# The end of a decoder layer on one Trainium2 core: the first half of the output written during the last product's steps, and the last three steps ordered by blocks of tokens

## The chip, the cores and the metric

The kernel runs on one core of a Trainium2 chip. The metric is the device time of one execution in microseconds; before the change the median of three runs is 2199.48 us (2195.65 to 2199.91). The profile comes from a further execution.

## The reference

One decoder layer over 512 tokens of width 2048 in float32: two groups of attention heads with a residual, then a SwiGLU feed-forward block with a residual. Only its last two lines matter here:

```
h = rmsnorm(x, g_pre_ffn[l]) * (1.0 + sc_f) + sh_f
f = (jax.nn.silu(h @ w_gate[l]) * (h @ w_up[l])) @ w_down[l]
x = x + gt_f * rmsnorm(f, g_post_ffn[l])
```

So the last product, by `w_down` (5632 x 2048), is followed by a mean of squares over all 2048 columns of a token, by a gain for each column, and by the residual. No element of a token's output can be written before all its columns are there.

## The kernel before

**Precision.** Every float32 operand of a product is split in two: `hi`, a rounded copy (ScalarE, line 1704), and `lo`, what is left (VectorE, line 1713). A product is three matmuls: activations hi by weights hi, hi by lo, lo by hi (lines 282 to 284). The matmul by `hi` of a step can therefore start before its `lo` is there, the next one can't.

**Steps.** All the work after the first stage is a list of steps, each with one 128x1024 tile of weights (512 KB). In step `i` the program issues on each engine, in this order: what was hung on the step's start, the step's first half of matmuls, `do_hi(i + 2)` on ScalarE, the second half of matmuls, what was hung on `post_ev`, `do_lo(i + 2)` on VectorE, then `post_end`, `d_sums` (sums of weight tiles on VectorE) and `d_load` (loads on SyncE's queue, line 1505 for activations, 1522 for weights). Each engine runs its own instructions strictly in that order. `w_hi` and `w_lo` have three buffers each, so `do_hi(i + 2)` waits until step `i - 1` has been read by TensorE.

**The last product.** Its 512 x 5632 by 5632 x 2048 is done by one level of a Strassen-like scheme with seven products instead of eight, for two halves `c` of the columns. Tokens are four blocks of 128: blocks 0 and 1 are the first token half, 2 and 3 the second. For each `c` the products come as `m1`, `P`, `R`, `Y2`, then `Q` and `m2` in turn, and at last `T`, eleven steps each. `dpos[c, name, j]` is the number of a step.  A step works on two blocks of tokens (`tb` 0 and 1) with 6 matmuls each, so it has 12 matmuls. With `N` the number of steps, the last eleven, `N-11` to `N-1`, are `T` of `c = 1`; step `N-12` is `m2, 10`. `T` adds only to the second token half of the second half of the columns (`q = 2`), so the first token half is complete after `m2`.

**Finishing.** `du` holds the product's rows in SBUF, one tile for each block of tokens. `d_copy` and `d_comb` (lines 1608, 1612) bring in PSUM's sums, `d_sq` (1625, ScalarE) squares with a sum over 512 columns, `rstd` (1152 to 1157; VectorE, then GpSimd) makes the factor of a token, `d_gain` (1630, VectorE) multiplies by the gains, and `d_out` (1654) does `du * rstd + x2` on VectorE and starts the write to DRAM (1655, mostly on SyncE's queue). `x2`, the residual, is read back from DRAM by `x2_load` (1659), into buffers `XTAGS` that hold weights until then.

**Order at the end.** The matmuls of the last `NLAST = 2` steps are kept back and ordered by blocks of tokens:

```
last = range(NSTEP - NLAST, NSTEP)
for tb in range(2):
    for q in range(2):
        d_out(tb, 1024 * q, 1024)
for tb in range(2):
    for i in last:
        steps[i]["mm"](*hl[i], tb)
    d_comb(1, 2, "R", OP.add, (tb,))
    ...
```

The four `d_out` of the first token half (128x1024 each) stand on VectorE behind the last `w_lo` and ahead of everything that the second half needs.

Of the kernel before, what the change touches and what calls it, by code (L numbers as in the profile page):

```python
# [34 lines left out]
def body(tc, t):  # L35
# [5 lines left out]
    with ctx:  # L41
# [272 lines left out]
        start_ev = defaultdict(list)  # L314
        pe_ev = defaultdict(list)
        mid_ev = defaultdict(list)
        post_ev = defaultdict(list)
# [341 lines left out]
        post_end = defaultdict(list)  # L659
# [288 lines left out]
        dseq, dpos = [], {}  # L948
# [31 lines left out]
        NSTEP = len(steps)  # L980
# [75 lines left out]
        for i in range(W0 + 60):  # L1056
# [24 lines left out]
            while ada_todo and i < W0 + 46 and i >= 1 and t_dve + 1.14 <= t_end + (M_ADA if i < W0 else M_ADAW) and \  # L1081
                    t_dma + 1.45 <= t_end + M_DMA and len(aux[i]) < NAUX:
                t_dma += 1.45
                n, ch, hf = ada_todo.pop(0)
# [42 lines left out]
        HF = {}  # L1127
# [21 lines left out]
        def rstd(ss, n):  # L1149

            if n > 1:
                dve.reduce_sum(ss[:, 5:6], ss[:, 0:n], axis=mybir.AxisListType.X)
                src = ss[:, 5:6]
            else:
                src = ss[:, 0:1]
            dve.tensor_scalar(ss[:, 6:7], src, 1.0 / D, EPS, op0=OP.mult, op1=OP.add)
            pool.tensor_tensor(ss[:, 7:8], ss[:, 6:7], mhalf[:, 0:1], op=OP.pow)
# [339 lines left out]
        def d_load(e):  # L1497
            while aloads and aloads[0][0] <= e:
                c, name, j = aloads[0][1:]
                p = apool.get()  # L1500
                assert p is not None, (e, aloads[0])
                aloads.pop(0)
                a_of[c, name, j] = p
                v = p[1].rearrange("p (h k t) -> p h k t", h=2, k=2)
                sync.dma_start(v, acts[ACOMBO[DP[name][0]], j])
                atile[c, name, j] = v.bitcast(R)
            while dloads and dloads[0][0] <= e:
                at, end, c, n, q, j = dloads[0]
                p = None
                if c == 1 and n == "C":  # L1510
                    p = rawp.get([u for u in ("raw", "R10", "R11", "P2", "P5", *STAGE_RAW) if u not in XTAGS])
                elif c == 1:
                    p = rawp.get(XTAGS)
                if p is None:
                    p = rawp.get()
                if p is None:
                    assert end > e, (e, dloads[0], len(apool.free))
                    break
                dloads.pop(0)
                draw_of[c, n, j] = p  # L1520
                draw[c, n, j] = p[1]
                sync.dma_start(p[1], adar[dots[j]] if n == "dot" else wds[c, q, j])
# [97 lines left out]
        def d_sq(c, q, tbs=(0, 1)):  # L1620
            if "t" not in sq:
                sq["t"] = U("R7", [128, 4, 512], name="sq")
            for tb in tbs:
                t_, cg = 2 * (q // 2) + tb, 2 * c + q % 2
                act.activation(sq["t"][:, tb, :], du(c, q, tb), AF.Square, accum_out=HF["dss", t_][:, cg:cg + 1])

        def d_gain(c, q, tbs=(0, 1)):
            for tb in tbs:
                u = du(c, q, tb)
                dve.tensor_tensor(u, u, GTG[1][:, 2 * c + q % 2, :], op=OP.mult)  # L1630

        for c in range(2):
            p = dpos
            post_ev[p[c, "m1", 10] + 1].append(lambda c=c: d_copy(c, 0, "m1"))
            post_ev[p[c, "P", 10] + 1].append(lambda c=c: d_copy(c, 3, "P"))
            post_ev[p[c, "Y2", 10] + 1].append(lambda c=c: d_c12(c))
            post_ev[p[c, "Y2", 10] + 2].append(lambda c=c: d_comb(c, 3, "R", OP.subtract))
            post_ev[p[c, "Q", 10] + 1].append(lambda c=c: (d_copy(c, 2, "m1"), d_comb(c, 1, "m1", OP.subtract)))
            post_ev[p[c, "m2", 10] + 1].append(lambda c=c: d_comb(c, 0, "m2", OP.add))
            post_ev[p[c, "m2", 10] + 2].append(lambda c=c: d_comb(c, 3, "m1", OP.subtract))  # L1640
            post_ev[p[c, "m2", 10] + 3].append(lambda c=c: (d_sq(c, 0), d_sq(c, 1)))
            post_ev[p[c, "m2", 10] + 4].append(lambda c=c: d_sq(c, 3))
            if c == 0:
                post_ev[p[c, "T", 10] + 1].append(lambda c=c: d_comb(c, 2, "R", OP.add))
                post_ev[p[c, "T", 10] + 2].append(lambda c=c: d_sq(c, 2))
# [1 line left out]
        for n, (c, q) in enumerate(((0, 0), (0, 1), (0, 2), (0, 3))):  # L1647
            post_end[gtf_end + 8 + 2 * n].append(lambda c=c, q=q: d_gain(c, q))
        for n, q in enumerate((0, 1, 3)):
            post_end[dpos[1, "m2", 10] + 5 + n].append(lambda q=q: d_gain(1, q))  # L1650

        def d_out(tb, c0, n):
            u = HF["du", tb].rearrange("p c n -> p (c n)")[:, c0:c0 + n]
# [3 lines left out]
        def x2_load(tb):  # L1657
            HF["x2", tb] = U(XTAGS[tb], [128, 2048], name=f"x2_{tb}")
            sync.dma_start(HF["x2", tb], x2d[tb])
        for tb in range(4):  # L1660
            start_ev[dpos[1, "T", 0] + 1 + tb].append(lambda tb=tb: x2_load(tb))
        for tb in range(2):
            post_end[NSTEP - 4].append(lambda tb=tb: rstd(HF["dss", tb], 4))


        LA = 2
# [100 lines left out]
            do_hi(i)  # L1767
            do_lo(i)

        NLAST = 2  # L1770
        for i in range(NSTEP):
            for f in start_ev[i]:
                f()
# [39 lines left out]
                d_more()  # L1813

        last = range(NSTEP - NLAST, NSTEP)
        for tb in range(2):
            for q in range(2):
                d_out(tb, 1024 * q, 1024)
        for tb in range(2):
            for i in last:  # L1820
                steps[i]["mm"](*hl[i], tb)
# [107 lines left out]
```

## Time and profile before

| | |
|---|---|
| median of 3 runs | 2199.48 us (2195.65 to 2199.91) |
| the profiled execution | 2196.76 us |
| its span, first to last instruction | 2195.0 us |
| TensorE busy (matmuls) | 2152.4 us, 98% |
| VectorE busy | 1668.9 us, 76% |
| ScalarE busy | 1058.3 us, 48% |
| GpSimd busy | 107.1 us, 5% |
| mean granted TensorE clock | 0.993 of full speed |

The span lies 1.76 us under the profiled execution's own time. Busy shares are means over the whole span; what holds the end is read from the last 45 us, step by step. A timeline row gives the start, the duration, engine, line, operation, what it writes and reads with the shape, the number of instructions merged in the row, and in brackets the idle time of the engine before it and who ended it. Rows of one engine overlap by some hundredths: the next VectorE instruction starts about 0.08 us before the row of the one ahead of it ends.

### The profile page before, as it was taken

Reading aid. Unit: us, or ns where it says so; the run is one execution under the profiler, and the core shown is the slowest. Engines: PE = TensorE matmul, PEld = TensorE weight load, DVE = VectorE, ACT = ScalarE, POOL = GpSimd, SP = SyncE. Lnnn points to the kernel's source line nnn. Section 1 sums busy time; section 2 is a strip of 40 time slices with the busy share of each in tenths; the row PEclk is TensorE's granted clock in tenths of the full one; section 3 lists DMA queues with packets and bytes.
Section 4 is the critical chain, followed back from the end, with each engine's and each line's share of the span. In section 5 each row is a group of like instructions: output and inputs, shape, how many; then the busy total and the mean of one; then the engine's idle time right before and its main releaser. Section 6 shows DMA issues by size and latency. Waiting matters only on the chain.

```text
span 2195.0 us, 26915 instructions
## 1 busy us (share of the span) xinstructions
PE 2152.4 (98%) x9748; PEld 1757.8 (80%) x9748; DVE 1668.9 (76%) x2333; ACT 1058.3 (48%) x1541; POOL 107.1 (5%) x116
## 2 busy tenths in 40 slices
PE   7999999999999999999999999999999999999997
PEld 6888777778888888777888888888888888888886
DVE  6987877776777676776777777776777788798888
ACT  5444344444435564644555554555555544444443
POOL 0000000001001000000001001000000000000000
PEclk8999999999999999999999999999999999999999
DMA  9797534545678877897778769778877889899996
GB/s 374 295 347 228 165 119 150 176 160 166 217 230 274 294 248 252 274 294 220 222 233 268 225 205 289 213 206 262 244 222 214 278 322 401 335 387 363 345 338 266
DMA packets 161028, 566.48 MB, mean 258 GB/s; under 512 B 17504, under 2 KB 17792, under 8 KB 154496
## 3 DMA queue, kind: packets, MB, share of 16 engines
q1 hardware_dynamic: 142608, 502.09, 63.8%
q0 software_dynamic: 11520, 41.95, 10.7%
q10 hardware_dynamic: 6768, 20.73, 3.1%
q8 instruction: 77, 1.26, 0.2%
q14 instruction: 55, 0.45, 0.1%
HBM read 501.77 MB, written 54.02 MB: 253 GB/s over the span
## 4 chain that ended last, share of the span: by engine, by line
PE 88%; DVE 5%; DMA 4%; ACT 1%; issue 1%; SPq 0%; POOL 0%; POOLq 0%; ACTq 0%; DVEq 0%
PE b L283 22%; PE b L282 22%; PE b L284 22%; PE b L277 6%; PE b L279 5%; PE b L278 5%; PE b L507 2%; DVE w_lo L1713 2%; DMA a<-acts 1%; PE b L545 1%; DMA raw<-in_wgu 1%; PE b L1276 1%; PE b L500 1%; PE b L529 1%; ACT w_hi L1704 1%
## 5 line engine op out<-in xcount | busy, mean ns | idle before, releaser
L1713 DVE TENSOR_TENSOR w_lo<-raw,w_hi 128x1024 fp32r<-128x1024 f32 x232 | 282.7, 1222 | 140.9 <-ACT w_hi L1704 140.7
L1704 ACT ACTIVATE w_hi<-raw 128x1024 fp32r<-128x1024 f32 x232 | 245.6, 1060 | 291.7 <-PE b L284 216.8
L282 PE MATMUL b<-w_hi,h 128*128 128x512 f32 x864 | 343.7, 398 | 2.3 <-ACT w_hi L1704 2.0
L283 PE MATMUL b<-w_lo,h 128*128 128x512 f32 x864 | 337.9, 391 | 4.1 <-DVE w_lo L1713 4.0
L284 PE MATMUL b<-w_hi,h 128*128 128x512 f32 x864 | 337.5, 391 | 0.0
L1713 DVE TENSOR_TENSOR w_lo<-w_raw,w_hi 128x1024 fp32r<-128x1024 f32 x176 | 214.2, 1221 | 61.3 <-ACT w_hi L1704 61.1
L1704 ACT ACTIVATE w_hi<-w_raw 128x1024 fp32r<-128x1024 f32 x176 | 185.2, 1055 | 142.7 <-PE b L284 58.3
L282 PE MATMUL b<-w_hi,e 128*128 128x512 f32 x640 | 249.9, 390 | 3.2 <-ACT w_hi L1704 3.2
L283 PE MATMUL b<-w_lo,e 128*128 128x512 f32 x640 | 250.1, 391 | 1.6 <-DVE w_lo L1713 1.6
L284 PE MATMUL b<-w_hi,e 128*128 128x512 f32 x640 | 249.7, 390 | 0.0
L283 PE MATMUL b<-w_lo,a 128*128 128x512 f32 x616 | 240.0, 390 | 1.1 <-DVE w_lo L1713 1.1
L282 PE MATMUL b<-w_hi,a 128*128 128x512 f32 x616 | 240.1, 390 | 1.0 <-DMA a<-acts 1.0
L284 PE MATMUL b<-w_hi,a 128*128 128x512 f32 x616 | 239.7, 389 | 0.0
L1704 ACT ACTIVATE w_hi<-w_lent 128x1024 fp32r<-128x1024 f32 x128 | 135.7, 1061 | 165.8 <-PE b L284 125.2
L1713 DVE TENSOR_TENSOR w_lo<-w_lent,w_hi 128x1024 fp32r<-128x1024 f32 x128 | 156.3, 1223 | 76.7 <-ACT w_hi L1704 76.7
L277 PE MATMUL b<-h,w_hi 128*128 128x512 f32 x512 | 213.3, 417 | 0.0
L278 PE MATMUL b<-h,w_hi 128*128 128x512 f32 x512 | 200.8, 392 | 2.5 <-DVE h L273 2.5
L279 PE MATMUL b<-h,w_lo 128*128 128x512 f32 x512 | 201.3, 393 | 0.0
L283 PEld LDWEIGHTS b<-w_lo,h 128*128 128x128 f32 x864 | 162.8, 188 | 39.8 <-DVE w_lo L1713 6.7
L282 PEld LDWEIGHTS b<-w_hi,h 128*128 128x128 f32 x864 | 162.6, 188 | 39.6 <-issue 3.7
L284 PEld LDWEIGHTS b<-w_hi,h 128*128 128x128 f32 x864 | 162.6, 188 | 34.2
L282 PEld LDWEIGHTS b<-w_hi,e 128*128 128x128 f32 x640 | 120.5, 188 | 28.5 <-ACT w_hi L1704 3.6
(348 smaller groups left out, 3448.1 us busy)
## 6 DMA issues: line engine op xcount, KB each, us to landing
a<-acts SPq DMA_DIRECT2D x154, 512.0 KB, 5.5
raw<-in_wgu SPq DMA_DIRECT2D x127, 512.0 KB, 6.6
w_raw<-in_win SPq DMA_DIRECT2D x107, 512.0 KB, 5.0
w_raw<-in_adar SPq DMA_DIRECT2D x96, 512.0 KB, 4.5
w_lent<-in_wgu SPq DMA_DIRECT2D x73, 512.0 KB, 6.2
w_raw<-in_wout SPq DMA_DIRECT2D x64, 512.0 KB, 4.8
raw<-in_wgu POOLq DMA_DIRECT2D x56, 512.0 KB, 7.0
raw<-in_wds SPq DMA_DIRECT2D x46, 512.0 KB, 6.2
```

The lines of the kernel that those rows point to most:

```text
L277: pe.matmul(ps, whi, ahi, start=start, stop=False, **kw)
L278: pe.matmul(ps, whi, alo, start=False, stop=False, **kw)
L279: pe.matmul(ps, wlo, ahi, start=False, stop=stop, **kw)
L282: pe.matmul(ps, ahi, whi, start=start, stop=False, **kw)
L283: pe.matmul(ps, ahi, wlo, start=False, stop=False, **kw)
L284: pe.matmul(ps, alo, whi, start=False, stop=stop, **kw)
L500: pe.matmul(sc[:, r], qk[:, i, qs], qk[:, i + 1, :N], start=True, stop=True)
L507: pe.matmul(sc[:, :N], qk[k, 2 * m, qs], qk[k, 2 * m + 1, :N], start=True, stop=True)
L529: pe.transpose(tr[:, j, :], misc["p"][:, n % 2, 128 * j:128 * j + 128], ident)
L545: pe.matmul(h["pv"][:, qb, :], d["pt"][:, o:o + 128], v[:, j, e], start=j == 0, stop=j == qb)
L1704: act.activation(hi, raw, AF.Copy)
L1713: dve.tensor_tensor(lo, raw, hi.bitcast(F), op=OP.subtract)
```

## The change

The diff does six things. `d_sq` of the product's first three quarters moves one step earlier, for both `c`. `d_gain(1, q)` moves two steps earlier, to steps `N-9`, `N-8`, `N-7`. `rstd` of blocks 0 and 1 moves from step `N-4` to `N-9`. The four `d_out` of the first token half leave the end and are hung on steps `N-7`, `N-6`, `N-5` and `N-4`, each behind that step's `do_lo`. The four loads of `x2` move from steps `N-10` to `N-7` to steps `N-22`, `N-20`, `N-18` and `N-16`; for that, late loads of weights take other buffers than `XTAGS`. Three steps instead of two are kept back and ordered by blocks of tokens.

```diff
-                elif c == 1:
+                elif c == 1 and n in ("B12", "B22"):
                     p = rawp.get(XTAGS)
+                elif at > dpos[1, "m2", 0] - 8:
+                    p = rawp.get([u for u in ("raw", "R10", "R11", "P2", "P5", *STAGE_RAW) if u not in XTAGS])
...
-            post_ev[p[c, "m2", 10] + 3].append(lambda c=c: (d_sq(c, 0), d_sq(c, 1)))
-            post_ev[p[c, "m2", 10] + 4].append(lambda c=c: d_sq(c, 3))
+            post_ev[p[c, "m2", 10] + 2].append(lambda c=c: (d_sq(c, 0), d_sq(c, 1)))
+            post_ev[p[c, "m2", 10] + 3].append(lambda c=c: d_sq(c, 3))
...
-            post_end[dpos[1, "m2", 10] + 5 + n].append(lambda q=q: d_gain(1, q))
+            post_end[dpos[1, "m2", 10] + 3 + n].append(lambda q=q: d_gain(1, q))
...
-            start_ev[dpos[1, "T", 0] + 1 + tb].append(lambda tb=tb: x2_load(tb))
+            start_ev[dpos[1, "m2", 5 + tb]].append(lambda tb=tb: x2_load(tb))
...
-            post_end[NSTEP - 4].append(lambda tb=tb: rstd(HF["dss", tb], 4))
+            post_end[dpos[1, "m2", 10] + 3].append(lambda tb=tb: rstd(HF["dss", tb], 4))
+            for q in range(2):
+                post_end[dpos[1, "m2", 10] + 5 + 2 * tb + q].append(lambda tb=tb, q=q: d_out(tb, 1024 * q, 1024))
...
-        NLAST = 2
+        NLAST = 3
...
-        for tb in range(2):
-            for q in range(2):
-                d_out(tb, 1024 * q, 1024)
```

The first place where instructions move is VectorE, up to the first `d_comb` of the end. `w_lo` is the splitting of a step's weights, `du_13991` and `du_13994` are blocks 0 and 1, `du_14070` and `du_14073` blocks 2 and 3, `gtg` the gains, `x_0` and `x_1` the residuals. Before, from the last but one `w_lo` on:

```order
L1713 TENSOR_TENSOR w_lo<-stage_7304,w_hi 128x1024
L1152 TENSOR_REDUCE dss<-dss 128x1
L1156 TENSOR_SCALAR dss<-dss 128x1
L1152 TENSOR_REDUCE dss<-dss 128x1
L1156 TENSOR_SCALAR dss<-dss 128x1
L1713 TENSOR_TENSOR w_lo<-w_lent,w_hi 128x1024
L1654 SCALAR_TENSOR_TENSOR du_13991<-du_13991,dss,x_0_16024 128x1024 x2
L1654 SCALAR_TENSOR_TENSOR du_13994<-du_13994,dss,x_1_16047 128x1024 x2
L1612 TENSOR_TENSOR du_14070<-du_14070,b_14806 128x512
```

And now, from the first output on:

```order
L1656 SCALAR_TENSOR_TENSOR du_13991<-du_13991,dss,x_0_15792 128x1024
L1717 TENSOR_TENSOR w_lo<-stageb,w_hi 128x1024
L1632 TENSOR_TENSOR du_14070<-du_14070,gtg_15898 128x512
L1632 TENSOR_TENSOR du_14073<-du_14073,gtg_15898 128x512
L1656 SCALAR_TENSOR_TENSOR du_13991<-du_13991,dss,x_0_15792 128x1024
L1717 TENSOR_TENSOR w_lo<-stage_6928,w_hi 128x1024
L1656 SCALAR_TENSOR_TENSOR du_13994<-du_13994,dss,x_1_15831 128x1024
L1717 TENSOR_TENSOR w_lo<-stage_7304,w_hi 128x1024
L1656 SCALAR_TENSOR_TENSOR du_13994<-du_13994,dss,x_1_15831 128x1024
L1717 TENSOR_TENSOR w_lo<-w_lent,w_hi 128x1024
L1614 TENSOR_TENSOR du_14070<-du_14070,b_14806 128x512
```

The four outputs, which stood behind the last `w_lo`, now stand one ahead of each of the last four (steps `N-4` to `N-1`), and two gains stand among them as before.

The second place is SyncE's queue at the end; `a` are activations, `x` the residual, `out` the output. Before:

```order
L1659 DMA x_3_16093<-x2d 128x2048
L1505 DMA a_13090<-acts 128x1024 x2
L1655 DMA out<-du_13991 128x1024 x2
L1655 DMA out<-du_13994 128x1024 x2
L1655 DMA out<-du_14070 128x512 x4
```

And now:

```order
L1661 DMA x_3_15917<-x2d 128x2048
L1505 DMA a_13091<-acts 128x1024
L1505 DMA a_13089<-acts 128x1024 x2
L1505 DMA a_13090<-acts 128x1024 x2
L1505 DMA a_13091<-acts 128x1024 x2
L1505 DMA a_13089<-acts 128x1024 x2
L1657 DMA out<-du_13991 128x1024
L1505 DMA a_13090<-acts 128x1024
L1657 DMA out<-du_13991 128x1024
L1505 DMA a_13090<-acts 128x1024
L1657 DMA out<-du_13994 128x1024 x2
```

The activations of steps `N-2` and `N-1` (`a_13090`, two halves of one buffer) now stand each behind a write of the output.

## Rows read from the trace of the kernel before

**Rows 1.** The page's head: the span, and each engine's busy time with its share and number of instructions.

```profile
span 2195.0 us, 26915 instructions
PE 2152.4 (98%) x9748; PEld 1757.8 (80%) x9748; DVE 1668.9 (76%) x2333; ACT 1058.3 (48%) x1541; POOL 107.1 (5%) x116
```

**Rows 2.** Busy time by windows of one step each (from one `w_hi` to the next; steps `N-10` and `N-9`, `N-6` to `N-3`, and the end): window and length, busy time of PE, PEld, DVE, ACT and POOL with their instructions, the granted clock, the share of the DMA engines, GB/s.

```profile
2153.61:2156.38 2.77, 2.77 (x13) 2.06 (x11) 2.77 (x4) 1.06 (x1) 0.00 (x0) 1.00 1.01 413
2156.38:2159.80 3.42, 3.05 (x14) 2.42 (x14) 3.42 (x6) 3.42 (x9) 0.00 (x0) 1.00 1.04 426
...
2165.16:2167.88 2.72, 2.72 (x13) 2.25 (x12) 2.66 (x4) 1.06 (x2) 0.00 (x0) 1.00 1.00 413
2167.88:2170.60 2.72, 2.72 (x13) 2.25 (x12) 2.72 (x5) 1.07 (x2) 0.00 (x0) 1.00 0.87 343
2170.60:2173.32 2.72, 2.72 (x13) 2.25 (x12) 2.72 (x5) 1.06 (x2) 0.00 (x0) 1.00 0.04 17
2173.32:2176.04 2.72, 2.72 (x13) 2.25 (x12) 2.11 (x7) 1.06 (x1) 1.08 (x2) 1.00 0.00 0
2176.04:2181.50 5.46, 5.40 (x24) 4.13 (x22) 4.98 (x5) 0.45 (x1) 0.00 (x0) 1.00 0.71 284
```

**Rows 3.** VectorE's timeline over the last 46 us.

```profile
2149.75 1.28 DVE L1612 TENSOR_TENSOR du<-du,b 128x512 f32<-128x512 f32 x2 [1.98 <-ACT du L1608]
...
2155.62 1.22 DVE L1713 TENSOR_TENSOR w_lo<-rawR,w_hi 128x1024 fp32r<-128x1024 f32 x1
...
2157.95 1.22 DVE L1713 TENSOR_TENSOR w_lo<-w_lent,w_hi 128x1024 fp32r<-128x1024 f32 x1
...
2160.29 1.23 DVE L1713 TENSOR_TENSOR w_lo<-stage,w_hi 128x1024 fp32r<-128x1024 f32 x1
...
2173.28 0.15 DVE L1152 TENSOR_REDUCE dss<-dss 128x1 f32<-128x4 f32 x1
...
2173.72 0.15 DVE L1156 TENSOR_SCALAR dss<-dss 128x1 f32<-128x1 f32 x1
2174.41 1.23 DVE L1713 TENSOR_TENSOR w_lo<-w_lent,w_hi 128x1024 fp32r<-128x1024 f32 x1 [0.54 <-ACT w_hi L1704]
2175.55 4.87 DVE L1654 SCALAR_TENSOR_TENSOR du<-du,dss,x 128x1024 f32<-128x1024 f32 x4
2180.34 0.68 DVE L1612 TENSOR_TENSOR du<-du,b 128x512 f32<-128x512 f32 x1
2185.85 0.68 DVE L1612 TENSOR_TENSOR du<-du,b 128x512 f32<-128x512 f32 x1
...
2188.71 2.74 DVE L1654 SCALAR_TENSOR_TENSOR du<-du,dss,x 128x512 f32<-128x512 f32 x4 [0.44 <-POOL dss L1157]
```

**Rows 4.** TensorE's timeline: the first matmul of step `N-9` and the next one, the first of step `N-3`, the first of the two steps kept back, the last of their first block of tokens, and the last of all.

```profile
2156.13 0.39 PE L282 MATMUL b<-w_hi,a 128*128 128x512 f32 x1
2156.89 0.50 PE L283 MATMUL b<-w_lo,a 128*128 128x512 f32 x1 [0.37 <-DVE w_lo L1713]
...
2173.12 0.39 PE L282 MATMUL b<-w_hi,a 128*128 128x512 f32 x1
...
2175.84 0.39 PE L282 MATMUL b<-w_hi,a 128*128 128x512 f32 x1
...
2178.33 0.39 PE L284 MATMUL b<-w_hi,a 128*128 128x512 f32 x1
...
2181.05 0.39 PE L284 MATMUL b<-w_hi,a 128*128 128x512 f32 x1
```

**Rows 5.** DMAs from issue to landing, shortest, median and longest: the activations over 2085 to 2196 us, the same over 2120 to 2150 us, and the writes of the output.

```profile
DMA to landing us min/median/max: 3.4/5.7/9.2
...
DMA to landing us min/median/max: 3.4/4.9/6.8
...
DMA to landing us min/median/max: 2.2/2.4/2.9
```

**Rows 6.** Busy time by windows, columns as in rows 2: the stretch of steps `N-23` to `N-17`, the one in which the residual is loaded before the change, and the one between the last load and the first write.

```profile
2118.10:2137.10 19.00, 19.00 (x86) 15.60 (x85) 15.10 (x19) 7.57 (x8) 0.00 (x0) 1.00 0.88 321
...
2151.00:2162.50 11.50, 11.13 (x50) 8.89 (x49) 11.50 (x15) 7.77 (x17) 0.00 (x0) 1.00 0.93 360
2170.60:2176.90 6.30, 6.30 (x29) 5.22 (x28) 5.69 (x11) 2.12 (x2) 1.08 (x2) 1.00 0.02 7
```

**Rows 7.** ScalarE's timeline where it writes the row of gains to DRAM and waits for it, and the `w_lo` behind that on VectorE.

```profile
2133.46 0.33 ACTq L1021 DMA_DIRECT2D rowd<-row  x1
...
2136.17 1.06 ACT L1704 ACTIVATE w_hi<-stage 128x1024 fp32r<-128x1024 f32 x1 [2.73 <-DMA rowd<-row]
...
2137.26 1.23 DVE L1713 TENSOR_TENSOR w_lo<-stage,w_hi 128x1024 fp32r<-128x1024 f32 x1 [2.11 <-ACT w_hi L1704]
```

**Rows 8.** TensorE's clock near the start: windows of 2 us (columns as in rows 2), the wait ahead of a transpose that falls among them, and two matmuls at the lower clock.

```profile
16.00:18.00 2.00, 0.00 (x0) 0.00 (x0) 1.27 (x7) 1.79 (x4) 0.55 (x1) 0.50 1.06 436
30.00:32.00 2.00, 0.73 (x6) 0.41 (x4) 2.00 (x4) 1.80 (x4) 0.00 (x0) 1.00 1.02 418
...
18.08 1.97 PE L207 MATMUL b<-cst,x_in 128*128 128x128 f32 x8 [4.10 <-DVE x_in L135]
...
25.23 0.63 PE L277 MATMUL b<-h,w_hi 128*128 128x512 f32 x1
25.65 0.63 PE L278 MATMUL b<-h,w_hi 128*128 128x512 f32 x1
```

## The prediction

> **What bounds the kernel now.** I read the page first: TensorE is busy for 2152.4 of 2195.0 us, VectorE for 76% [rows 1]. By that mean VectorE has room for anything. The change touches only the last 75 us, so next come windows of one step each: in steps N-10 and N-9 VectorE is busy for the whole window, and from N-6 to N-4 for 2.66 to 2.72 of 2.72 us [rows 2]. Here VectorE has no room. In the same rows TensorE loses time only in N-9 (3.05 busy of 3.42 us). Then VectorE's timeline [rows 3]: from 2149.75 on it waits for next to nothing (11.50 busy of 11.50 us up to 2162.5 [rows 6], 0.06 us free in N-6), then for 0.54 us on the last `w_hi`; the four outputs of the first token half follow (2175.55, 4.87 us in all), and at 2180.34 the first `d_comb` of the second half. TensorE ended that block's matmuls at 2178.33 + 0.39 = 2178.72 and all of them at 2181.44 [rows 4]. So the end is VectorE's: block 2 waits 1.6 us for it, block 3 4.4 us. From `d_comb` to `d_comb` is 5.51 us (2180.34 to 2185.85), the second chain ends at 2191.45, and the span 3.55 us later, with the last write and the closing. That the end hangs on VectorE is what invites the change. What the reader is to see is that the place to which the work goes is VectorE's as well.
>
> **The change, part by part.**
>
> *The outputs on VectorE.* Four of about 1.20 us each (2175.55 to 2180.34) leave the end and come ahead of the last four `w_lo`. The work between 2149.75 and the last `w_lo` is otherwise the same, only its order changes: two pairs of gains and the two `rstd` come earlier. Where VectorE has no idle time, order does not change when a list of work is done. I follow the new order with the row's own pitches: `w_lo` 1.14 (2174.41 to 2175.55), a pair of `du` operations 1.20 (2155.62 to 2157.95 holds one and a `w_lo`), two `rstd` 0.6 (2173.28 to 2173.87). Up to `w_lo` of N-7 at 2160.29 nothing changes. Then gains 2161.43, `rstd` 2162.63, `w_lo` N-6 2163.25, four gains, `w_lo` N-5 2166.8, gains, output, `w_lo` N-4 2170.3, gains, output, `w_lo` N-3 2173.9, output, `w_lo` N-2 2176.2, output, `w_lo` N-1 2178.6, ended at 2179.8.
>
> *What TensorE makes of it.* It needs a step's `w_lo` from the step's second matmul on. Step N-3 began at 2173.12 [rows 4], a step takes 2.72 us, so N-5, N-4 would begin at 2167.68 and 2170.40. `w_lo` N-5 ends at 2168.0 (0.1 late for a second matmul at 2167.91), N-4 at 2171.5 (0.8 late), N-3 at 2175.1 (a further 0.8), N-2 and N-1 1.0 each: about 3.7 us in which TensorE stands, where it stands for none now. Row 2156.89 [rows 4] is such a stop: 0.37 us, ended by `w_lo`, at the only place where VectorE is behind now.
>
> *The start of the last chain.* With the last `w_lo` at 2179.8, five matmuls of block 2 are left: four pitches of 0.227 us (2175.84 to 2178.33 is eleven) and 0.39 us of the last, so `d_comb` starts at 2181.2 instead of 2180.34. Block 3's 18 matmuls end 4.1 us later, at 2185.2; VectorE is with block 2 until 2181.2 + 5.5 = 2186.7, so they lie beside it. The second chain starts at 2186.7 instead of 2185.85. **The sum is +0.9 us**: 4.8 us of outputs taken away, 4.8 us of the same outputs put ahead of the last `w_lo`, 0.6 us of idle time filled, and 1.4 us of matmuls that the outputs used to cover now stand bare.
>
> *Three steps kept back.* The last block needs 18 instead of 12 matmuls after block 2's; these are covered as shown, with 1.5 us to spare. Had every `w_lo` been there in time, block 2 would be ready at 2173.12 + 17 x 0.227 + 0.39 = 2177.4, and the gain 2.9 us (2180.34 less 2177.4); that is the lower end for this part.
>
> *Squares one step earlier.* ScalarE does four of them ahead of the `w_hi` of N-7 instead of behind it. They take what is left of its 3.42 us in N-9 beside a `w_hi` of 1.06, 2.4 us [rows 2]; so that `w_hi`, which starts at 2156.38 now, ends at 2159.8 at the latest, and its `w_lo` starts at 2160.29 because VectorE is busy until then. Nothing; the first half of the columns has the same order.
>
> *The residual loads.* Four of 1 MB move on SyncE's queue from 2151 to 2160 us to 2121 to 2137 us, the first of them past twelve loads of activations and two of weights. That stretch moves 321 GB/s at a DMA share of 0.88; 4.2 MB more in 19 us would be 541, and the full rows show 413 to 426 [rows 2, 6]. So about 2.3 MB slip behind, 5.5 us of work, and activations land that much later than their 4.9 to 6.8 us [rows 5]: up to 12.3. They are issued five steps, 13.6 us, ahead. Nothing on the path; above, 1 us if one takes 9.2 + 5.5.
>
> *The row of gains.* It is written on ScalarE's queue at 2133.46 while a residual is in flight, and ScalarE stands 2.73 us for it [rows 7]. The `w_lo` behind it ends at 2138.5; its step N-15 needs it at 2156.13 - 6 x 2.72 + 0.23 = 2140.0, so 1.5 us more cost nothing. Between no more than now and the longest landing of a load here (9.2 us [rows 5], 6.5 more than the wait, so 5.0 of loss) I take nothing, since it is 8 KB. The Trainium skill (DMA: Bandwidth & Descriptors, Queues, rings and completion order) says that a DMA engine takes turns between queues, a packet at a time; by that the small write is not held behind SyncE's loads and the term is nothing. The wait of 2.73 us among loads now agrees; no run here shows it under a residual.
>
> *The last activations.* Those of N-2 and N-1 now stand on SyncE's queue behind outputs 1 and 2, so N-1's is issued when VectorE ends output 2, at about 2174.0, with the write ahead of it: 2174.6. It costs nothing if it lands within 5 us, by the time that `w_lo` N-1 is there. Here loads take 3.4 to 9.2 us [rows 5], the long ones at a full DMA; between 2170.6 and 2176.9 the share is 0.02 [rows 6]. I take 4.5 and nothing; the end above is 9.2, +4.2 us.
>
> **Result.** The profiled execution takes 2196.76 us, its span 2195.0. +0.9 gives 2197.7. The median shown is 2199.48, 2.7 above the profiled one; the middle of all four executions is 2198.1, and with 0.9 that is **2199.0 us**. 0.2%, 4.4 us, is about what a measurement of this kernel can tell from no change; the four executions alone spread over 4.3.
>
> **Rivals.** *The outputs find room* (10%): the end becomes free, 2193.8 on the profiled execution, 2195.2 on the middle. For it speaks the 76%; against it, the windows and the timeline, step by step [rows 2, 3]. The Trainium skill (the same page, Rules for kernel authors) advises to issue a DMA early and wait for it late; by that rule alone writing half the output early would give this time. The trace agrees that writes are hidden (2.2 to 2.9 us to landing [rows 5]), but what the writes wait for is VectorE.
>
> *The last activations come late* (8%, slower). The write of output 2 and the load behind it share a queue, and the load lands at 2174.6 plus its time. It decides from 5.0 us on. At the median of 5.7 the last chain starts 0.7 us later (2198.3), at 9.2 us 4.2 later (2201.9). For it: half a megabyte of output ahead of it on its queue. Against it: an all but idle DMA.
>
> *A transfer further ahead* (6%, slower): the row of gains or an activation load behind the residuals stops TensorE. 2 to 5.0 us more, so 2199.7 to 2202.7. It decides from 1.5 us more and from 13.6 us on.
>
> *The clock* (4%, slower). Near the start the granted clock stands at 0.50, the 1.2 GHz level, in a window without any matmul, inside a wait of 4.10 us; in a window that is busy for 0.73 of 2.00 us it is at 1.00, the 2.4 GHz level [rows 8]. So stops of 0.8 to 1.0 us should not lower it. If they did, the matmuls would come at 0.42 us (25.23 to 25.65) instead of 0.227: block 2's last five 1.0 us later, block 3's 18 in 7.6 us, beyond VectorE's 5.5: 2.1 more. 2200.8. The Trainium skill (TensorE: Matmul & The Clock Gate, A second HAM failure mode: psum-queue depth-cycling) tells of a kernel in which frequent short idles between groups of matmuls made the clock swing between its levels; by that rule this rival would come true. The stop of 0.37 us in N-9 left the granted clock at 1.00 [rows 2], against the rule; a run of several stops is not in these rows.
>
> **Numbers.** Forecast 72%, rivals 10, 8, 6 and 4. The forecast's own range, with the executions' spread, is 2196.6 to 2200.8. Range: below, 2195.2 of the first rival less 2.1, half the spread: 2193.1; above, 2200.8 plus 2.5, half of the most that a slow rival adds: 2203.3. Faster by over 0.2%: no case reaches it but through the spread: 0.07. Slower by over 0.2%: the slow rivals' upper ends, and the spread: 0.08. Within: 0.85.
>
> **What would show it.** Right: VectorE without a gap from 2149.75 to the end of the last `w_lo` at about 2179.8; four stops of TensorE of 0.8 to 1.0 us on `w_lo` from N-4 on; the first late `d_comb` at about 2181.2, the second 5.5 us behind it; the DMA share between 2170.6 and 2176.9 far above 0.02, with writes. Wrong: a first `d_comb` near 2177.4 (the first rival); stops of TensorE ended by a DMA in the last three steps or near 2140; a granted clock under 1.00 in the last 25 us; VectorE idle between outputs.

## The result, and the profile after

The change takes **2200.86 us** (median of 14 runs, 2196.86 to 2205.19), the kernel before 2196.18 in the same runs (14; 2193.13 to 2200.35): ratio 1.0021, 95% interval 1.0013 to 1.0028. It is slower by 4.7 us (2.9 to 6.1), where I had forecast +0.9, no change that can be measured. The profiled execution takes 2200.78 us, its span is 2199.0 (before: 2195.0 [rows 1]).

I read where TensorE waits first, since it alone has no spare time. Its waits over the last 115 us, first of the kernel before, then of the changed one (in us: total, number, longest):

```profile
PE b L283 <- DVE w_lo L1713: 0.4, 1, 0.4
```

```profile
PE b L282 <- DMA a<-acts: 3.7, 1, 3.7
PE b L283 <- DVE w_lo L1717: 2.9, 6, 0.7
```

Of the changed kernel's two lines the second is what was forecast. The first is not: one stop on activations. TensorE's timeline finds it, far ahead of the end, in step `N-13`; the small stop ahead of it is in `N-15`:

```profile
2136.12 0.39 PE L282 MATMUL b<-w_hi,a 128*128 128x512 f32 x1
2136.81 0.50 PE L283 MATMUL b<-w_lo,a 128*128 128x512 f32 x1 [0.30 <-DVE w_lo L1717]
...
2141.97 0.39 PE L284 MATMUL b<-w_hi,a 128*128 128x512 f32 x1
2146.06 0.77 PE L282 MATMUL b<-w_hi,a 128*128 128x512 f32 x1 [3.70 <-DMA a<-acts]
2146.62 0.63 PE L283 MATMUL b<-w_lo,a 128*128 128x512 f32 x1
...
2151.31 0.40 PE L282 MATMUL b<-w_hi,a 128*128 128x512 f32 x1
```

From 2136.12 to 2151.31 there are 36 matmul pitches, which at 0.227 us would be 8.2 us and here are 15.2: **7.0 us lost**. The stop is 3.9 of them (2141.97 to 2146.06 less a pitch). Behind it twelve pitches take 5.25 us instead of 2.72: 2.5 lost to the clock. The small stop at 2136.81 and its slow neighbour are 0.6. The windows show the clock (window and length, busy time of PE, PEld, DVE, ACT, POOL with instructions, the granted clock, DMA share, GB/s):

```profile
2132.00:2134.00 2.00, 2.00 (x10) 1.65 (x10) 0.00 (x0) 0.00 (x0) 0.00 (x0) 1.00 0.06 23
...
2142.00:2144.00 2.00, 0.36 (x2) 0.00 (x0) 1.88 (x2) 1.15 (x2) 0.00 (x0) 1.00 0.84 315
2144.00:2146.00 2.00, 0.00 (x0) 0.00 (x0) 1.62 (x2) 0.00 (x0) 0.00 (x0) 0.62 1.05 397
2146.00:2148.00 2.00, 1.94 (x5) 1.59 (x6) 0.00 (x0) 0.00 (x0) 0.00 (x0) 0.50 0.98 408
...
2152.00:2154.00 2.00, 2.00 (x10) 1.69 (x9) 0.92 (x2) 1.54 (x3) 0.00 (x0) 1.00 0.94 352
```

The granted clock falls while TensorE stands, stays at 0.50 (the 1.2 GHz level) after it has resumed, and is back at 1.00 from 2152 on. The first row is the telling one: ahead of the stop, from 2132 to 2134, the DMA engines are at 0.06. Before the change the stretch up to 2137 has 0.88 [rows 6]. Loads were wanted and not issued. So the next view is SyncE's queue, and ScalarE's timeline beside it:

```profile
2122.74 2.86 SPq L1505 DMA_DIRECT2D a<-acts  x2
2134.09 0.33 SPq L1524 DMA_DIRECT2D rawP<-in_wds  x1
2134.47 0.43 SPq L1661 DMA_DIRECT2D x<-x2d  x1
2134.99 6.14 SPq L1505 DMA_DIRECT2D a<-acts  x2
```

```profile
2129.77 0.33 ACTq L1021 DMA_DIRECT2D rowd<-row  x1
2134.03 0.35 ACTq L1026 DMA_DIRECT2D gtg<-rowd  x1
2134.43 1.06 ACT L1708 ACTIVATE w_hi<-stage 128x1024 fp32r<-128x1024 f32 x1 [4.69 <-DMA rowd<-row]
```

SyncE issues nothing from 2125.6 to 2134.09, and its waits name whom it stood for:

```profile
SPq L1524 <- DMA rowd<-row: 8.4, 1, 8.4
SPq L1505 <- DMA gtg<-rowd: 5.4, 1, 5.4
```

A load of weights waited 8.4 us for the row of gains to be written, though it has no data in common with it. The next load of activations on the queue is the one that TensorE stood for (step `N-13`). Five steps of 2.72 us ahead of 2142.2, where that step would have begun, is 2128.6; it was issued at 2134.99, 6.4 us later. It then took 10.9 us to land, with 2.5 MB (gains, weights and a residual) issued in the microsecond ahead of it (DMAs issued from 2134 to 2136: number, size, time to landing):

```profile
x<-x2d SPq DMA_DIRECT2D x1, 1024.0 KB, 10.2
...
a<-acts SPq DMA_DIRECT2D x1, 512.0 KB, 10.9
```

The load behind the second wait, of 5.4 us, is for step `N-12`. It landed at about 2147.2, 4 us ahead of that step (2151.31), but only because the stop had moved the step back: without the stop it would have begun at 2144.9 and have waited in its turn.

The list of waits in the built program says why SyncE stood. DMAs of SyncE and ScalarE get eight completion semaphores, DMAHW0 to 7, in turn over both engines in the order of that list, and a DMA that gets one waits first for the DMA that had it before. ScalarE's two, and SyncE's loads around them, in the changed kernel:

```
1300 L1021 DMA rowd_161<-row_15885 16x128 [waits DMAHW2_49,Activation_49]
1301 L1026 DMA gtg1_15898<-rowd_161 128x2048 [waits DMAHW5_49,DMAHW2_49]
...
903 L1661 DMA x2_0_15792<-x2d_162 128x2048 [waits DMAHW1_49]
904 L1505 DMA a6_13091<-acts_159 128x1024 [waits DMAHW3_49,PE_49]
...
907 L1661 DMA x2_1_15831<-x2d_162 128x2048 [waits DMAHW7_49,DVE_49]
...
910 L1524 DMA rawP5_13095<-in_wds 128x1024 [waits DMAHW2_49,DVE_49,Activation_49]
...
913 L1505 DMA a6_13091<-acts_159 128x1024 [waits DMAHW5_49,PE_49]
```

The write takes DMAHW2 between SyncE's loads 903 and 904, so load 910 waits for it; the load of the gains takes DMAHW5, so load 913 waits for that. In both kernels six of SyncE's loads lie between the write and the one that waits for it. Before, the seventh is a load of activations, which has to wait for TensorE anyway; SyncE stood for the write for 0.9 us:

```profile
SPq L1505 <- DMA rowd<-row: 0.9, 1, 0.9
```

In the changed list the write stands right behind the first residual and two loads of activations further forward, and the second residual is among the six. So the seventh is a load of weights, which SyncE reaches 4.2 us before ScalarE has even issued the write.

The end itself went as forecast. VectorE's timeline, as [rows 3] has it before:

```profile
2153.09 1.29 DVE L1614 TENSOR_TENSOR du<-du,b 128x512 f32<-128x512 f32 x2 [7.47 <-ACT du L1610]
...
2163.63 1.22 DVE L1717 TENSOR_TENSOR w_lo<-stage,w_hi 128x1024 fp32r<-128x1024 f32 x1
...
2181.75 1.22 DVE L1717 TENSOR_TENSOR w_lo<-w_lent,w_hi 128x1024 fp32r<-128x1024 f32 x1
2184.48 0.69 DVE L1614 TENSOR_TENSOR du<-du,b 128x512 f32<-128x512 f32 x1 [1.52 <-PE b L284]
2190.00 0.68 DVE L1614 TENSOR_TENSOR du<-du,b 128x512 f32<-128x512 f32 x1
```

The first of these rows stands 3.34 us later than its like before (2149.75 [rows 3]); that is the 7.0 us less 3.7 by which this execution was ahead at 2087.86 (below). The first late `d_comb` is 4.14 later than before and the second 4.15: **the end costs 0.8 us**, forecast 0.9.

### The profile page after: what moved, and what is told of

The parts are those of the page before. It is cut to its first block, busy times and chain, and to the rows that moved or that the text cites. A ratio compares the mean times of both kernels' runs of the same rounds, so it can differ in the third digit from the quotient of the medians.

```text
span 2199.0 us, 26910 instructions
## 1 busy us (share of the span) xinstructions
PE 2155.8 (98%) x9748; PEld 1757.9 (80%) x9748; DVE 1668.3 (76%) x2333; ACT 1058.9 (48%) x1541; POOL 108.0 (5%) x116
## 3 DMA queue, kind: packets, MB, share of 16 engines
q8 instruction: 77, 1.26, 0.2%
## 4 chain that ended last, share of the span: by engine, by line
PE 86%; DVE 6%; DMA 6%; ACT 1%; issue 1%; SPq 0%; POOL 0%; POOLq 0%; DVEq 0%; ACTq 0%
PE b L283 21%; PE b L282 21%; PE b L284 21%; PE b L277 6%; PE b L279 5%; PE b L278 5%; PE b L507 2%; DVE w_lo L1717 2%; DMA a<-acts 2%; DMA w_raw<-in_wout 1%; PE b L545 1%; DMA acts<-stage 1%; PE b L1276 1%; PE b L500 1%; PE b L529 1%
## 5 line engine op out<-in xcount | busy, mean ns | idle before, releaser
L1717 DVE TENSOR_TENSOR w_lo<-raw,w_hi 128x1024 fp32r<-128x1024 f32 x221 | 268.9, 1221 | 130.4 <-ACT w_hi L1708 130.3
L1708 ACT ACTIVATE w_hi<-raw 128x1024 fp32r<-128x1024 f32 x221 | 233.8, 1060 | 269.8 <-PE b L284 197.9
```

The costliest lines, as they stand in the source:

```text
L1708: act.activation(hi, raw, AF.Copy)
L1717: dve.tensor_tensor(lo, raw, hi.bitcast(F), op=OP.subtract)
```

## The experiments

The runs of one kernel spread over 3 to 10 us, and much of that arises elsewhere: the sum of product `Y2` for `c = 1` (L1616 before, L1618 after), ahead of all the late work, starts anywhere from 2087.86 to 2092.50 us in the thirteen traces. So beside the medians I use the stretch from that row to the first late `d_comb`, each from its own trace. Each ratio is to the kernel before on the same chip, whose medians were 2196.18 with the change, 2196.51 with the next four, 2196.96 with the four after them and 2196.38 with the last three.

| kernel | median us | ratio, 95% interval | `Y2` sum | late `d_comb` | stretch | less before's |
|---|---|---|---|---|---|---|
| before | 2196.18 | | 2091.55 | 2180.34 | 88.79 | |
| the change | 2200.86 | 1.0021 (1.0013 to 1.0028) | 2087.86 | 2184.48 | 96.62 | +7.8 |
| loads back | 2196.87 | 1.0000 (0.9991 to 1.0009) | 2091.18 | 2181.43 | 90.25 | +1.5 |
| loads alone | 2201.49 | 1.0020 (1.0011 to 1.0029) | 2089.87 | 2183.61 | 93.74 | +5.0 |
| loads from GpSimd | 2198.89 | 1.0013 (1.0004 to 1.0022) | 2092.18 | 2184.23 | 92.05 | +3.3 |
| row from GpSimd | 2196.72 | 1.0002 (0.9994 to 1.0011) | 2092.50 | 2182.08 | 89.58 | +0.8 |
| two outputs in gaps | 2196.25 | 0.9999 (0.9991 to 1.0008) | 2090.16 | 2178.86 | 88.70 | -0.1 |
| gains on GpSimd | 2198.70 | 1.0009 (1.0000 to 1.0018) | 2088.81 | 2180.24 | 91.43 | +2.6 |
| late gains left out | 2194.52 | 0.9989 (0.9980 to 0.9999) | 2091.26 | 2177.22 | 85.96 | -2.8 |
| before, row from GpSimd | 2196.35 | 0.9999 (0.9990 to 1.0008) | 2090.60 | 2179.43 | 88.83 | 0.0 |
| three outputs late | 2194.39 | 0.9992 (0.9983 to 1.0001) | 2090.39 | 2177.82 | 87.43 | -1.4 |
| gaps, writes from GpSimd | 2196.29 | 1.0002 (0.9993 to 1.0010) | 2090.71 | 2178.36 | 87.65 | -1.1 |
| three late, loads back | 2193.91 | 0.9989 (0.9980 to 0.9998) | 2089.80 | 2177.21 | 87.41 | -1.4 |

### Where the 4.7 us come from: four kernels

**Loads back.** The change, with the residual loads at their old steps.

```diff
-            start_ev[dpos[1, "m2", 5 + tb]].append(lambda tb=tb: x2_load(tb))
+            start_ev[dpos[1, "T", 0] + 1 + tb].append(lambda tb=tb: x2_load(tb))
```

> The change with the four residual loads back at their old steps (N-10 to N-7), all else kept. Medians so far: before 2196.2, the change 2200.9 us. Theory A (the row of gains and SyncE's queue): the loss near 2146 comes from SyncE standing on a completion semaphore that its loads share with the write and the load of the row of gains, and only the moved residual loads brought that wait forward; so no stop of TensorE on activations near 2146, granted clock 1.00 there, and only the end's +0.8: 2197.0 us. Theory B (bandwidth: the residuals fill the DMA engines, so activations land late whatever the queue does): the same, 2197.0. Theory C (the end costs it all, the stop near 2146 belongs to the one profiled execution): 2200.9. The end itself, by all: last w_lo to first late d_comb as in the change, 2.7 to 2.8 us from start to start, last chain 5.5 us.

2196.87, no stop on activations in the last 115 us. Theory C falls: without the moved loads the loss is gone. The stops on `w_lo` are those of the change; its row of waits for them, 2.9 us in six stops, is the same.

**Loads alone.** The kernel before, with the residual loads at the new steps and the new rule on buffers (the first hunk of the diff).

> The kernel before with only the four residual loads moved early and the rule on the weights' buffers that goes with it; outputs, gains, squares and the two steps kept back as before. A and B: SyncE stands for 8 and 5 us between N-20 and N-15, TensorE stops there for about 3.7 us on activations and the clock drops behind it; the end as before. 3.9 us more than before (4.7 less the end's 0.8): 2200.1 us; by the one profile of the change, up to 7 us more, 2203. C: 2196.2, no difference.

2201.49, all of the loss without any of the early outputs; C falls a second time. Its waits:

```profile
SPq L1524 <- DMA rowd<-row: 8.5, 1, 8.5
SPq L1505 <- DMA gtg<-rowd: 5.3, 1, 5.3
```

```profile
PE b L282 <- DMA a<-acts: 2.4, 1, 2.4
PE b L283 <- DVE w_lo L1715: 0.7, 2, 0.4
```

The stop is 2.4 us here and 3.7 in the change's trace, so it varies, and the one profiled execution of the change seems to be a dear one: 5.0 and 7.8 us of stretch against 5.0 and 4.7 of medians.

**Loads from GpSimd.** The change, `x2_load` issued on GpSimd's queue.

```diff
-            sync.dma_start(HF["x2", tb], x2d[tb])
+            pool.dma_start(HF["x2", tb], x2d[tb])
```

> The change with the four residual loads issued at the same steps from GpSimd's queue, which has completion semaphores of its own, so that SyncE's loads share theirs with the row of gains six loads later in the program again, as before the change. The bytes and about the times of the residuals are those of the change. A: SyncE no longer stands between N-20 and N-15, no stop near 2146, 2197.0 us. B: activations are late by the same bandwidth, the stop stays: 2200.9. C: 2200.9.

Between the two: 2198.89. SyncE's waits, and TensorE's:

```profile
SPq L1505 <- DMA a<-acts: 6.8, 5, 3.4
SPq L1505 <- DMA rowd<-row: 2.7, 1, 2.7
```

```profile
PE b L282 <- DMA a<-acts: 1.9, 2, 1.3
```

The wait of 8.4 us is gone, 2.7 is left, as with the loads back (2.8); in the built program's list the write stands where it stood before the change. ScalarE still stands for the write, for 5.45 us against 4.69 in the change, so it is not ScalarE's wait that made the stop near 2146. But B was not wholly wrong in this form: the activations take 9.4 us to land (median of 2110 to 2160 us) and two of them are late, by 1.26 and 0.64 us. The residuals go out on a queue of their own here, and also up to 5.6 us earlier than from SyncE's queue in the next kernel (2114.59 against 2120.20 for the first, two together at 2125.22); which of the two makes the activations late is not shown.

**Row from GpSimd.** The change, the second row of gains written and loaded on GpSimd's queue.

```diff
-                act.dma_start(rowd[which], row)
+                (act if which == 0 else pool).dma_start(rowd[which], row)
...
-                act.dma_start(GTG[which].rearrange("p a n -> p (a n)"), bass.AP(
+                (act if which == 0 else pool).dma_start(GTG[which].rearrange("p a n -> p (a n)"), bass.AP(
```

> The change with the write and the load of the second row of gains issued from GpSimd's queue instead of ScalarE's; the residual loads as in the change, on SyncE's queue. SyncE's loads then share no completion semaphore with the row, and ScalarE no longer stands for its landing. A: SyncE's two waits of 8.4 and 5.4 us go, no stop near 2146: 2197.0 us. B: the stop stays, 2200.9. C: 2200.9.

2196.72, as A has it. The residuals are at the steps where the change put them, and the DMA engines are fuller than in the change at the critical place:

```profile
2132.00:2134.00 2.00, 2.00 (x11) 1.59 (x10) 1.64 (x5) 1.06 (x1) 0.00 (x0) 1.00 1.00 410
2134.00:2140.00 6.00, 6.00 (x28) 4.94 (x27) 3.99 (x4) 2.39 (x3) 0.55 (x1) 1.00 1.02 415
```

Activations take 7.8 us to land (median; the longest 13.3), and none stops TensorE, whose waits over the last 115 us are one line:

```profile
PE b L283 <- DVE w_lo L1717: 2.6, 5, 0.7
```

So bandwidth alone, with the residuals in SyncE's own order, costs nothing: B falls, and A stands. Of the change this kernel keeps the end, and shows +0.8 us of stretch for it. The control, **the kernel before with the same move of the row**, tells that the move is worth nothing by itself:

> The kernel before with the second row of gains written and loaded from GpSimd's queue, nothing else. ScalarE's wait of 2.73 us goes, but TensorE waited for nothing there: by all theories 2196.5 us, as before. If ScalarE's wait did cost, up to 0.7 us less.

2196.35 and 0.0 us of stretch.

### Whether VectorE is what holds the end: three kernels

All start from the kernel with the row on GpSimd's queue.

**Late gains left out.** The output then lacks these gains.

```diff
-        for n, q in enumerate((0, 1, 3)):
-            post_end[dpos[1, "m2", 10] + 3 + n].append(lambda q=q: d_gain(1, q))
```

> The kernel with the row of gains on GpSimd's queue, without the six late gains (q 0, 1 and 3 of the second half of the columns), which leaves their factor out of the output. This frees 3.6 us of VectorE ahead of the last w_lo and adds nothing elsewhere. V: the stops on w_lo go, no stop of TensorE in the last 25 us, first late d_comb 2.6 us earlier: 2194.1 us. P: 2196.7.

2194.52; in the trace 3.6 us come off the stretch (89.58 to 85.96), a microsecond more than expected and just the time of the six operations. In the last 115 us one stop is left:

```profile
PE b L283 <- DVE w_lo L1715: 0.4, 1, 0.4
```

VectorE's list decided. I had expected only the 2.6 us of stops in the row of waits; a stop costs more than its bracket. In the change a `w_hi` matmul starts at 2181.95 and the next at 2183.02, 0.84 us more than a pitch, where the bracket says 0.62, and the one behind takes a further 0.11 (2183.02 to 2183.36):

```profile
2181.95 0.45 PE L282 MATMUL b<-w_hi,a 128*128 128x512 f32 x1
2183.02 0.50 PE L283 MATMUL b<-w_lo,a 128*128 128x512 f32 x1 [0.62 <-DVE w_lo L1717]
2183.36 0.39 PE L284 MATMUL b<-w_hi,a 128*128 128x512 f32 x1
```

**Gains on GpSimd.** The same six operations, done there, and the early outputs ordered by columns instead of by blocks.

```diff
-                dve.tensor_tensor(u, u, GTG[1][:, 2 * c + q % 2, :], op=OP.mult)
+                (pool if c == 1 and q != 2 else dve).tensor_tensor(u, u, GTG[1][:, 2 * c + q % 2, :], op=OP.mult)
...
-                post_end[dpos[1, "m2", 10] + 5 + 2 * tb + q].append(lambda tb=tb, q=q: d_out(tb, 1024 * q, 1024))
+                post_end[dpos[1, "m2", 10] + 5 + 2 * q + tb].append(lambda tb=tb, q=q: d_out(tb, 1024 * q, 1024))
```

> The kernel with the row of gains on GpSimd's queue, with the six late gains of the second half of the columns (128x512 each, q 0, 1 and 3) done by GpSimd instead of VectorE, and the early outputs in the order block 0, block 1 of the first columns, then of the second. V: 3.6 us leave VectorE's list ahead of the last w_lo, so the stops of TensorE on w_lo (2.6 us in the trace) go: 2194.1 us. That holds if GpSimd takes under some 2.5 us for one; no trace here shows such an operation on GpSimd, so it is open whether outputs then wait for it, in which case 2196.7 or more. P: 2196.7.

2198.70, and 1.9 us more stretch than with the gains on VectorE: the relief turned into a loss. The last four of GpSimd's gains, and VectorE's rows beside and behind them:

```profile
2161.89 7.53 POOL L1632 TENSOR_TENSOR du<-du,gtg 128x512 f32<-128x512 f32 x4
```

```profile
2163.74 2.31 DVE L1717 TENSOR_TENSOR w_lo<-rawR,w_hi 128x1024 fp32r<-128x1024 f32 x1
2165.97 2.31 DVE L1656 SCALAR_TENSOR_TENSOR du<-du,dss,x 128x1024 f32<-128x1024 f32 x1
...
2172.82 1.21 DVE L1717 TENSOR_TENSOR w_lo<-stage,w_hi 128x1024 fp32r<-128x1024 f32 x1
```

While GpSimd works, each 128x1024 operation of VectorE takes 2.31 instead of 1.21 us.

**Two outputs in gaps.** Block 1's outputs leave the place ahead of the last `w_lo` for VectorE's idle time behind it.

```diff
-                post_end[dpos[1, "m2", 10] + 5 + 2 * tb + q].append(lambda tb=tb, q=q: d_out(tb, 1024 * q, 1024))
+            post_end[dpos[1, "m2", 10] + 5 + q].append(lambda q=q: d_out(0, 1024 * q, 1024))
...
+        d_out(1, 0, 1024)
         for tb in range(2):
             for i in last:
                 steps[i]["mm"](*hl[i], tb)
             d_comb(1, 2, "R", OP.add, (tb,))
             d_sq(1, 2, (tb,))
+            d_out(1, 1024 + 512 * tb, 512)
```

> The kernel with the row of gains on GpSimd's queue (2196.7 us, profiled span 2196.7), with only block 0's two outputs early; block 1's stand at the end, one 128x1024 ahead of the first late d_comb, where VectorE stood idle for 1.50 us, and two 128x512 behind the two d_comb, where it stood for 0.79 us each on ScalarE's squares. Theory V (VectorE's list of work sets the end; its idle time lies behind the last w_lo): 2.4 us leave the list ahead of the last w_lo and land in 3.1 us of idle time, the first late d_comb 2.4 us earlier, the chains still 5.5 us apart: 2194.3 us, faster than before. Rival P (TensorE's order and stops set the end, VectorE's outputs are hidden anyway): 2196.7, no change. Rival W (writes: four more writes at the end queue ahead of the last ones): up to 1 us back, 2195.3.

Missed: 2196.25, and 0.9 us of stretch instead of 2.4. The outputs did fit (the chains stay 5.52 us apart), and the writes cost nothing (rival W): from the first late `d_comb` to the end of the span it is 14.6 us here and with all four outputs early. But TensorE, less held by `w_lo`, ran into the next thing:

```profile
2177.20 0.47 PE L282 MATMUL b<-w_hi,a 128*128 128x512 f32 x1 [0.77 <-DMA a<-acts]
```

```profile
2172.46 0.34 SPq L1657 DMA_DIRECT2D out<-du  x1
2172.89 0.39 SPq L1505 DMA_DIRECT2D a<-acts  x1
```

The last activations stand on SyncE's queue behind a write that waits for VectorE. This is the rival of the late last activations, which the change itself hides behind VectorE.

### Fewer outputs early: three more kernels

**Gaps, writes from GpSimd.** As the last one, with `d_out(0, 1024 * q, 1024, pool)` for the two early outputs, where the new last argument is the queue of the write.

> The kernel with two outputs early and two in the gaps, with the two early writes issued from GpSimd's queue instead of SyncE's. There the load of the last activations stood on SyncE's queue behind the second write (issued 2172.89 in that trace) and TensorE stopped 0.77 us for it. If that order was the cause, the load goes out two to three us earlier, the stop goes, and the end comes 0.8 us earlier: 2195.4 us. If the load is late by bandwidth, no change: 2196.2.

No stop on activations is left, and the stretch is 1.05 us shorter (88.70 to 87.65), as expected; the medians, 2196.29 and 2196.25, don't show a difference of that size.

**Three outputs late.** One output early, its write on GpSimd's queue; two ahead of the first late `d_comb`, one in the two gaps.

```diff
-            for q in range(2):
-                post_end[dpos[1, "m2", 10] + 5 + 2 * tb + q].append(lambda tb=tb, q=q: d_out(tb, 1024 * q, 1024))
+        post_end[dpos[1, "m2", 10] + 5].append(lambda: d_out(0, 0, 1024, pool))
...
+        d_out(0, 1024, 1024)
+        d_out(1, 0, 1024)
         for tb in range(2):
...
+            d_out(1, 1024 + 512 * tb, 512)
```

> The kernel with the row of gains on GpSimd's queue, with one output early (block 0, first columns; its write on GpSimd's queue, so that no activations stand behind it), two 128x1024 behind the last w_lo ahead of the first late d_comb, and the last one as two 128x512 in the two gaps of 0.79 us. Theory V: 3.6 us leave VectorE's list ahead of the last w_lo, as in the run without the late gains, where the stops on w_lo shrank from 2.6 to 0.4 us; 2.4 of them go into the time between the last w_lo and the first d_comb (1.5 us idle, and 1.2 more since the w_lo come earlier than TensorE can use them), 1.4 into the gaps. No stop by a DMA. First late d_comb 3.3 to 3.6 us earlier than with all four outputs early, 2193.2 us, faster than before. Rival (activations late whatever the queue): 0.8 us more, 2194.0. Rival P: 2196.7.

2194.39. In the trace 2.2 us come off, not 3.3 to 3.6. `w_lo` now waits for TensorE (by way of `w_hi`) and VectorE has no gap behind it:

```profile
2174.28 1.23 DVE L1716 TENSOR_TENSOR w_lo<-w_lent,w_hi 128x1024 fp32r<-128x1024 f32 x1 [0.54 <-ACT w_hi L1707]
2175.42 2.47 DVE L1656 SCALAR_TENSOR_TENSOR du<-du,dss,x 128x1024 f32<-128x1024 f32 x2
2177.82 0.68 DVE L1614 TENSOR_TENSOR du<-du,b 128x512 f32<-128x512 f32 x1
```

I had let the last `w_lo` move by the full 3.6 us; it can't start before its `w_hi`, and behind it the matmuls left to do cover 1.5 us of outputs (the idle time elsewhere), not 2.4. **Three late, loads back** is the same with the residual loads at their old steps:

> The kernel with three outputs late, and the residual loads back at their old steps N-10 to N-7. If nothing at the end needs the residuals early, it takes the same time: 2193.2 us. The one early output needs its residual 8 us after its issue; loads of a residual took 7.0 to 8.8 us to land, so at most 0.7 us more, 2193.9.

2193.91, ratio 0.9989 (0.9980 to 0.9998): by the ratio 2.4 us faster than before (0.4 to 4.4, so the interval only just leaves out no change), and by both ratios some 7 faster than the change. The early loads of the residual were worth nothing to it.

## Why the prediction was wrong, point by point

- **The number is close by luck.** 2199.0 is 1.9 us from the measured median because I started from 2198.1, the middle of four executions, where the median of 14 is 2196.18. The step itself was +0.9 in the forecast and is +4.7.
- **The outputs on VectorE, and the last chain: right.** Counted from the row that stands 3.34 us later, I had the last `w_lo` end at 2179.8 + 3.3 = 2183.1 (measured 2181.75 + 1.22 = 2183.0) and the two `d_comb` start at 2184.5 and 2190.0 (2184.48 and 2190.00). VectorE had no gap in between. The kernel with the row on GpSimd's queue isolates this term: +0.8, forecast +0.9.
- **TensorE's stops at the end: right in place and nearly in size.** I gave 0.1 us at `N-5` and four stops of 0.8 to 1.0 from `N-4` on, 3.7 together. The brackets are 0.48, 0.50, 0.68 and 0.62; against the pitch, reckoned as above, TensorE lost 0.75, 0.77, 0.95 and 0.96, 3.4 together, and nothing at `N-5`.
- **Squares: nothing**; the +0.8 leaves no room for more. **The last activations: nothing** in the change; 0.8 us once the outputs no longer covered them.
- **The residual loads: the failed step.** "Nothing on the path" was argued by bandwidth, and by bandwidth it held, if narrowly: with the row moved off ScalarE's queue the same loads, at a DMA share of 1.00 to 1.02, stop nobody, and activations take up to 13.3 us to land, where I had given 12.3 and a lead of 13.6. What failed is the list of what the moved loads touch. I counted what they are moved past on SyncE's queue, and not what their place in the program does to the semaphores that they share with ScalarE's DMAs: SyncE stood 8.4 us for the write of the row, and a load of activations went out 6.4 us late. The loss measured for it is 4 to 5 us (in medians 4.7 of the change less 0.2 of the kernel with the row moved, and 5.0 for the loads alone), against nothing in the sum.
- **The row of gains: also wrong as a term.** I took nothing for a later landing. It took 4.2 us instead of 2.3, ScalarE stood 4.69 instead of 2.73, and the 0.6 us that TensorE loses at 2136.81 in `N-15` is about what my point of decision (1.5 us more) gives for 1.96. The Trainium skill (DMA: Bandwidth & Descriptors, Queues, rings and completion order) has each DMA engine take turns between the queues, a packet at a time, from which I had concluded that the 8 KB are free. The traces don't bear out the conclusion: the write took 4.2 to 5.0 us in all nine traces with the residual loads moved and 4.2 with the loads back, against 2.3 before, 1.7 in the control and 1.7 in the last kernel.
- **The rival "a transfer further ahead"** named the place and the size (2 to 5 us), at 6%. Its mechanism was another: I had it decide from a landing of 13.6 us on. The load took 10.9 and stopped TensorE all the same, since it was issued late.
- **The clock: half right.** Short stops did not lower it: over the ten microseconds with the stops at the end the granted clock is 1.00. That is unlike the kernel with frequent short idles of which the Trainium skill (TensorE: Matmul & The Clock Gate, A second HAM failure mode: psum-queue depth-cycling) tells and which the prediction weighed.

```profile
2174.00:2184.00 10.00, 7.73 (x30) 5.12 (x29) 8.96 (x9) 2.12 (x2) 0.00 (x0) 1.00 0.87 313
```

  The 3.70 us stop did lower it, as the wait of 4.10 us near the start had [rows 8]. In the kernel with the loads alone the stop of 2.4 us did so too (0.50 from 2148 to 2150); with the loads from GpSimd the stops of 1.26 and 0.64 us did not (1.00 in every window of 2 us from 2138 to 2152). I priced the clock only for the end; behind the stop it cost 2.5 us.

What stays open: why the write of the row lands in 2.3 us in the trace of before and in 4.2 with the loads back, where no residual is in flight either (one trace each). The rule on buffers is what these two differ in at that place; it was not tried alone. By itself it does not slow the write on GpSimd's queue: the last kernel has the new rule and the residuals at their old steps, and there the write takes 1.7 us as in the control. In the kernel with the loads back TensorE loses 0.6 us in `N-15`, as in the change; that is most of the 0.7 by which its +1.5 of stretch stands above the end's own +0.8.

## What to carry to other kernels

When a DMA is moved in a program, list what it does to the others' completion semaphores as well as to queues and bytes: where a few are handed out in turn, a load can stand for a transfer of another engine that it has no data in common with, and its whole queue behind it. Here an idle DMA system (0.06) just ahead of a stop on data meant that loads had not been issued; the waits of the issuing queue are the place to look first. Work that is to be hidden goes where the engine is idle in the timeline, and not to where its mean over the span says that it has room.

## What had not been expected of the hardware

Element-wise work on GpSimd beside VectorE: four 128x512 multiplications took 1.88 us each there, and VectorE's 128x1024 operations took 2.31 instead of 1.21 us in that time. VectorE lost 1.1 us on each of three of them and as much on a pair of gains (2.38 instead of 1.28), 4.4 together, where the four multiplications would have cost it 2.4. The Trainium skill (SBUF — State Buffer, Who interferes with whom) says that a VectorE instruction with two inputs in SBUF contends with a GpSimd instruction that reads SBUF; the traces agree, at nearly a factor of two.
